# A two-layer hybrid decoder trunk: the up weights' sums in two tiles with three copies of the transferred half, and the down products added onto the residual by GpSimd

## The chip, the cores and the metric

The kernel runs on one core of a Trainium2 chip. A core has TensorE (PE in the profile; its weight loads are listed apart as PEld), VectorE (DVE), ScalarE (ACT), GpSimd (POOL) and SyncE (SP), which each work through their own instructions in order and wait for one another by semaphores. SBUF holds 128 partitions of data; PSUM holds what TensorE writes. The metric is the device time of one execution in microseconds (us). Before the change three runs took 1287.45, 1287.9 and 1292.94 us (median 1287.9).

## The reference, cut to what matters

Two layers run over 528 rows (16 learned rows ahead of 512 tokens) of width 1024. Each layer normalises, projects, mixes by two kinds of attention heads, adds the result to `h`, and then runs a gated feed-forward network, the only part that the change touches:

```python
hn = rmsnorm(h, ffn_norm_g)
ff = jax.nn.silu(jnp.einsum('bld,df->blf', hn, w_gate)) * jnp.einsum('bld,df->blf', hn, w_up)
return h + jnp.einsum('blf,fd->bld', ff, w_down)
```

`w_gate` and `w_up` are 1024 x 2816, `w_down` is 2816 x 1024, everything in float32. After the last layer `h` is normalised again and the 16 learned rows are dropped.

## The kernel before

Activations lie transposed: `h[0]` to `h[7]` are SBUF tiles of 128 features by 528 rows. Each float32 operand of a product is split into a high part of TensorE's own float32r format and a low part (the rest), and a product takes three matmuls: high by high, high by low, low by high. So each weight block needs, after it has landed, a cast on ScalarE (the high part, `whi` or `fwhi`) and a subtraction on VectorE (the low part, `wlo` or `fwlo`); `splits` (L885) does both.

**The feed-forward network.** The 2816 hidden features are 22 blocks of 128, in six rounds (`ROUNDS`). The first three blocks of a layer are computed plainly. Each of the other 19 is a `Unit`: its gate block and its up block together are a 2x2 product of half blocks, done with seven half products instead of eight (a Strassen scheme), so that sums of weight halves are needed as well as the weights. A `Down` does the same for two blocks of output features and four hidden blocks of the round before. From the third round on, units (called far) and Downs alternate, so that TensorE always has products of both kinds.

**A unit's weights.** `load` (L919) takes four transfers and adds in flight: `raw` (`t["a"]`) is the gate block, 128 x 1024; `fraw` (`t["b"]`) is the up block, onto whose first half the first half of the gate block is accumulated by a transfer of GpSimd's queue (L927); `Sw` (`t["s"]`) is a tile of 128 x 1024 of which the transfers fill the second half alone: the second half of the up block comes through SyncE (L925), and onto it a transfer of GpSimd's queue accumulates the first half (L926). `make1` to `make4` then make the four sets of split weights of the unit: `make1` from `raw`; `make2` from `Sw`, once VectorE has put the sum of its second half and of the first half of `raw` into its first half (L935), by one cast (L936) and one subtraction (L937) over 1024 columns; `make3` from `fraw`; `make4` from the last sum, which a far unit puts in `Sw`'s first half right behind L937 (L939), and another unit puts in `raw` when `make4` comes (L951). There are two `Sw` tiles, so the transfers for a unit wait until `make4` of the unit two before has read its tile. `raw` has three tiles, which Downs use too, `fraw` two. Tiles of split weights come in four pairs that jobs use in turn, and `need` (L880) asks for the next three or four jobs ahead.

**A Down's results.** `load` (L1049) fetches two blocks of `w_down` and lets GpSimd make sums of weights, six operations on 128 x 128 pieces (L1057, L1059, L1061). The products go through ScalarE copies (L1089) and VectorE sums (L1091, L1107) into a tile `S` of five rows; `add` (L1096) then adds two of these rows onto an `h` tile. For 15 of the 16 Downs of a layer this is a transfer of GpSimd's queue from `S` to `h` that accumulates (L1100); the last uses VectorE (L1102).

**What sets the order.** TensorE's order is the program's (`plan`, written out by hand). On the other engines a scheduler orders what is ready, except for pieces that are pinned or raised (`keep_in_program_order`, `high_priority`); the result is a fixed list for each engine, and whatever waits at the head of a list holds up all that stands behind it.

Of the kernel before, what the change touches and what calls it, by code (L numbers as in the profile page):

```python
# [10 lines left out]
F32 = mybir.dt.float32  # L11
F32R = mybir.dt.float32r
AF = mybir.ActivationFunctionType
ALU = mybir.AluOpType

D = 1024
NK = D // 128
# [11 lines left out]
HB = NK // 2  # L29
# [10 lines left out]
def hybrid_kernel(ctx, tc, x_t, w_in, w_fl, w_out, w_gate, w_up, w_down, vecs, b_fg, rope, decay, mask, ident, out_t):  # L40
    nc = tc.nc
# [9 lines left out]
    h = [state.tile([128, T], F32, name=f"h{k}") for k in range(NK)]  # L51
# [221 lines left out]
    def fft(tag, dt=F32R, shape=(128, T), bufs=None):  # L273
        return phase["ffn"].tile(list(shape), dt, name=tag, tag=tag, bufs=bufs)
# [519 lines left out]
    def ffn(l, st, real, last):  # L794
# [8 lines left out]
        def two(t):  # L803
            return t[:, t0:T].rearrange("p (a b) -> p a b", a=2)
# [80 lines left out]
        def splits(hi, lo, src):  # L885
            nc.scalar.copy(hi, src)  # L886
            nc.vector.tensor_sub(lo, src, hi.bitcast(F32))  # L887
# [17 lines left out]
        class Unit:  # L905
# [13 lines left out]
            def load(self):  # L919
                if "a" not in self.t:  # L920
                    for n, src, pool, tag, bufs in (("a", w_gate, wp, "raw", 3), ("b", w_up, phase["ffn"], "fraw", 2)):
                        self.t[n] = pool.tile([128, NK, 128], F32, name=tag, tag=tag, bufs=bufs)
                        nc.sync.dma_start(self.t[n], src[l, self.f])
                    s = self.t["s"] = fft("Sw", F32, (128, NK, 128), 2)
                    nc.sync.dma_start(s[:, HB:NK], w_up[l, self.f][:, HB:NK])  # L925
                    nc.gpsimd.dma_start(s[:, HB:NK], w_up[l, self.f][:, 0:HB], accum_op=ALU.add)  # L926
                    nc.gpsimd.dma_start(self.t["b"][:, 0:HB], w_gate[l, self.f][:, 0:HB], accum_op=ALU.add)  # L927

            def make1(self, hi, lo):
# [2 lines left out]

            def make2(self, hi, lo):
                a, s = self.t["a"], self.t["s"]
                nc.vector.tensor_add(s[:, 0:HB], s[:, HB:NK], a[:, 0:HB])  # L935
                nc.scalar.activation(hi, s, AF.Copy, scale=-1.0)  # L936
                nc.vector.scalar_tensor_tensor(lo, s, -1.0, hi.bitcast(F32), ALU.mult, ALU.subtract)  # L937
                if self.far:
                    nc.vector.tensor_add(s[:, 0:HB], a[:, HB:NK], s[:, 0:HB])  # L939


            def make3(self, hi, lo):
                splits(hi, lo, self.t["b"])


            def make4(self, hi, lo):
                a, s = self.t["a"], self.t["s"]
                if self.far:
                    splits(hi, lo, s[:, 0:HB])
                else:  # L950
                    nc.vector.tensor_add(a[:, HB:NK], a[:, HB:NK], s[:, 0:HB])  # L951
                    splits(hi, lo, a[:, HB:NK])

            def bank(self, n):
                def go():
# [82 lines left out]
        class Down:  # L1038
# [57 lines left out]
            def add(self, s):  # L1096
                m = 2 * self.m + s
                e = self.t["e"][:, 2 * s:2 * s + 2]
                if self.dma:
                    nc.gpsimd.dma_start(two(h[m]), e, accum_op=ALU.add)  # L1100
                else:
                    nc.vector.tensor_add(two(h[m]), e, two(h[m]))  # L1102

# [16 lines left out]
        def down_job(p, f0, f1):  # L1120

            n = f1 - f0
            t = {}

            def load():
                if t:
                    return
                t["r"] = wp.tile([128, NK, 128], F32, name="raw", tag="raw", bufs=3)
                for s in range(2):
                    nc.sync.dma_start(t["r"][:, s * n:s * n + n], w_down[l, 2 * p + s, :, f0:f1])  # L1130

            return add_job(load=load, make=lambda hi, lo: splits(hi, lo, t["r"][:, 0:2 * n]), n=2 * n)
# [40 lines left out]
        for r, (f0, f1) in enumerate(ROUNDS):  # L1173
            for f in range(f0, f1):
# [5 lines left out]
                if r > 1 and fills:  # L1180
                    p = fills.pop(0)[0]
                    if p == 0:
                        u.rest()
                        d = Down(p, r - 1, True)
# [3 lines left out]
                    else:  # L1188
                        d = Down(p, r - 1, True)
                        u.rest()  # L1190
                        d.second()
                        if f == NF - 1:
                            e = Down(fills.pop(0)[0], r - 1, False)
# [203 lines left out]
    def layer(l):  # L1397
# [80 lines left out]
        for g in range(2):  # L1478
# [15 lines left out]
                      ret_places(3, 52, 45.5, 47.5, 57.5, 55.5, 58.5, 60, 64.1, 63, 64.2))  # L1494
        plan += [op[3], op[7], op[11], op[15]] + op[16:]
        up = ffn(l, ff, real, real)
        plan += [lambda: enter("ffn"), start_ffn] + up
        return plan
# [79 lines left out]
```

## Time and profile before

| | before |
|---|---|
| runs | 1287.45, 1287.9, 1292.94 us (median 1287.9) |
| profiled execution, its own time | 1293.39 us |
| its span, first to last instruction | 1291.6 us |
| mean granted TensorE clock | 0.989 |
| busy share of the span: PE, DVE, ACT, POOL | 97%, 80%, 60%, 42% |
| DMA, mean | 132 GB/s, 170.80 MB |

A page of the profile gives busy times by engine, the span in 40 slices, the DMA queues, the chain of work that ended last and the costliest groups of instructions. Other views answer questions: the waits (who waited for whom), the chain in order of time, the timeline of an engine, one tile's or one line's instructions (minimum, median and maximum duration), and windows (busy time and number of instructions of each engine in a stretch, with the granted clock and the DMA share). L12 is line 12 of the kernel. The feed-forward network runs from about 314 to 640 us in the first layer and from about 960 to 1260 us in the second.

### The profile page before, as it was taken

How to read it: one execution, taken by the hardware profiler on the slowest of the kernel's cores; microseconds unless marked ns; L12 is line 12 of the kernel's file. 1: busy time of each engine (PE TensorE's matmuls, PEld its weight loads, DVE VectorE, ACT ScalarE, POOL GpSimd, SP SyncE). 2: the span in 40 equal slices, each digit the busy share in tenths (PEclk: the TensorE clock that was granted, in tenths of full speed). 3: DMA queues.
4: the chain of work that ended last, by engine and by line, in shares of the span. 5: the costliest groups of instructions: out<-in, count | busy, mean ns of one | idle time of the engine just before them, and what ended most of it. 6: DMA issues, size and time to landing. Idle time of an engine off the chain costs nothing. (4 is left out here: it accounts for less than half of the span.)

```text
span 1291.6 us, 25256 instructions
## 1 busy us (share of the span) xinstructions
PE 1251.1 (97%) x9463; PEld 1203.4 (93%) x9463; DVE 1032.3 (80%) x1942; ACT 780.5 (60%) x1534; POOL 544.4 (42%) x866
## 2 busy tenths in 40 slices
PE   9999999999999999899999999999999998999996
PEld 8999999999999999899899988998788998999986
DVE  7877756779678888798886877477887897999976
ACT  6666555776555556466556665457655665666654
POOL 3355645511134445355325545554102454555540
PEclk9999999999999999999999999999999999999998
DMA  6222223125776767686523232221457767778841
GB/s 216 95 78 83 83 75 91 50 87 155 175 185 151 183 165 183 145 207 165 131 75 117 70 96 82 83 79 61 139 152 182 171 162 182 180 191 193 200 104 65
DMA packets 73050, 170.80 MB, mean 132 GB/s; under 512 B 8400, under 2 KB 15312, under 8 KB 72928
## 3 DMA queue, kind: packets, MB, share of 16 engines
q1 hardware_dynamic: 50576, 128.70, 30.4%
q0 software_dynamic: 21888, 40.17, 19.3%
q8 instruction: 74, 1.21, 0.4%
q14 instruction: 48, 0.39, 0.1%
q10 hardware_dynamic: 464, 0.32, 0.1%
HBM read 146.79 MB, written 2.13 MB: 115 GB/s over the span
## 5 line engine op out<-in xcount | busy, mean ns | idle before, releaser
L194 POOL TENSOR_TENSOR wlo<-raw,whi 128x128 fp32r<-128x128 f32 x504 | 258.2, 547 | 284.7 <-ACT whi L191 284.6
L217 PE MATMUL psd<-xh,whi 128*128 128x264 f32 (+1 forms) x792 | 196.3, 315 | 0.5 <-ACT whi L191 0.5
L217 PE MATMUL psd<-xh,wlo 128*128 128x264 f32 (+1 forms) x792 | 187.1, 304 | 0.0
L217 PE MATMUL psd<-xl,whi 128*128 128x264 f32 (+1 forms) x792 | 186.6, 303 | 0.4 <-DVE xl L320 0.4
L217 PEld LDWEIGHTS psd<-xh,whi 128*128 128x128 f32 x792 | 128.8, 190 | 5.6 <-ACT whi L191 1.3
L217 PEld LDWEIGHTS psd<-xh,wlo 128*128 128x128 f32 x792 | 127.5, 189 | 6.3 <-DVE wlo L194 0.4
L217 PEld LDWEIGHTS psd<-xl,whi 128*128 128x128 f32 x792 | 128.1, 189 | 4.8 <-DVE xl L320 0.8
L191 ACT CAST whi<-raw 128x512 fp32r<-128x512 f32 (+1 forms) x168 | 98.4, 613 | 49.1 <-PE psd L217 37.0
L1100 POOL DMA_DIRECT2D h<-S x60 | 60.6, 1042 | 93.9 <-ACT S L1089 32.7
L886 ACT CAST whi<-raw 128x1024 fp32r<-128x1024 f32 (+2 forms) x68 | 62.7, 929 | 47.6 <-PE psd L898 26.1
L887 DVE TENSOR_TENSOR wlo<-raw,whi 128x1024 fp32r<-128x1024 f32 (+2 forms) x68 | 75.8, 1116 | 17.1 <-ACT whi L886 16.8
L926 POOL DMA_DIRECT2D Sw<-w_up x38 | 37.1, 975 | 111.8 <-DVE wlo L887 40.1
L898 PE MATMUL psa<-th,fwhi 128*128 128x264 f32 (+1 forms) x256 | 73.9, 289 | 1.7 <-ACT e L970 1.7
L898 PE MATMUL psa<-tl,fwhi 128*128 128x264 f32 (+1 forms) x256 | 73.4, 287 | 0.0
L898 PE MATMUL psa<-th,fwlo 128*128 128x264 f32 (+1 forms) x256 | 73.2, 286 | 0.0
L142 ACT CAST ab<-tq 128x528 fp32r<-128x528 f32 (+1 forms) x64 | 36.1, 573 | 60.4 <-DVE tq L988 31.3
L970 ACT COPY e<-psa 128x264 f32<-128x264 f32 (+1 forms) x114 | 42.7, 374 | 41.4 <-PE psa L898 41.2
L898 PE MATMUL psa<-ab,fwhi 128*128 128x264 f32 (+3 forms) x304 | 60.9, 290 | 5.7 <-ACT S L1089 5.3
L898 PE MATMUL psd<-xh,whi 128*128 128x264 f32 (+1 forms) x192 | 55.5, 289 | 8.6 <-DVE sg L980 5.4
L935 DVE TENSOR_TENSOR Sw<-Sw,raw 128x512 f32<-128x512 f32 x38 | 27.1, 713 | 45.8 <-DMA raw<-w_gate 23.3
L527 ACT ACTIVATE probs<-probs,nmax 128x144 f32<-128x144 f32 (+1 forms) x64 | 36.9, 576 | 44.4 <-DVE nmax L514 31.5
L927 POOL DMA_DIRECT2D fraw<-w_gate x38 | 33.5, 883 | 68.7 <-DVE wlo L194 21.9
(367 smaller groups left out, 4502.1 us busy)
## 6 DMA issues: line engine op xcount, KB each, us to landing
raw<-w_in SPq DMA_DIRECT2D x54, 512.0 KB, 3.5
raw<-w_gate SPq DMA_DIRECT2D x44, 512.0 KB, 5.8
fraw<-w_up SPq DMA_DIRECT2D x38, 512.0 KB, 6.1
raw<-w_down SPq DMA_DIRECT2D x64, 256.0 KB, 4.4
h<-S POOLq DMA_DIRECT2D x38, 264.0 KB, 5.7
Sw<-w_up SPq DMA_DIRECT2D x38, 256.0 KB, 3.7
fraw<-w_gate POOLq DMA_DIRECT2D x38, 256.0 KB, 4.2
Sw<-w_up POOLq DMA_DIRECT2D x38, 256.0 KB, 5.8
```

The source lines that it names most:

```text
L142: pin(nc.scalar.copy(hi, src), pinned)
L191: pin(nc.scalar.copy(hi, job["raw"][:, c0:c1]), pinned)
L194: pin(sub(lo[:, i:i + step], job["raw"][:, c0 + i:c0 + i + step], hi[:, i:i + step].bitcast(F32)), pinned)
L217: nc.tensor.matmul(ps[1][b][:, 0:c1 - c0], w[:, wk, :], x[:, c0:c1], start=(k == 0 and i == 0), stop=(k == n - 1 and i == 2))
L527: nc.scalar.activation(pr, pr, AF.Exp, bias=nmax[0:nq], scale=-1.0, accum_out=rsum)
L886: nc.scalar.copy(hi, src)
L887: nc.vector.tensor_sub(lo, src, hi.bitcast(F32))
L898: nc.tensor.matmul(bank()[:, 0:b.shape[-1]], a[:, o + k, :], b, start=(fresh and k == 0 and i == 0), stop=(k == n - 1 and i == 2), skip_gr ...
L926: nc.gpsimd.dma_start(s[:, HB:NK], w_up[l, self.f][:, 0:HB], accum_op=ALU.add)
L927: nc.gpsimd.dma_start(self.t["b"][:, 0:HB], w_gate[l, self.f][:, 0:HB], accum_op=ALU.add)
L970: nc.scalar.copy(self.t["e"][:, i], self.t["x"][:, 0:w])
L1100: nc.gpsimd.dma_start(two(h[m]), e, accum_op=ALU.add)
```

## The change

The sum of `Sw`'s second half and `raw` now goes to a tile of its own, `Sd` (128 x 512, one of it), and `Sw` keeps only the transferred half, 128 x 512, in three tiles. Together they take as much SBUF as the two tiles took. `make2` therefore casts and subtracts in two pieces of 512 columns, `make4` reads `Sd` in every unit, and `raw` is read for the last time in `make2` in every unit. In `add`, the transfer is replaced by an addition on GpSimd, from `S` and `h` in SBUF onto `h`.

```diff
-                    s = self.t["s"] = fft("Sw", F32, (128, NK, 128), 2)
-                    nc.sync.dma_start(s[:, HB:NK], w_up[l, self.f][:, HB:NK])
-                    nc.gpsimd.dma_start(s[:, HB:NK], w_up[l, self.f][:, 0:HB], accum_op=ALU.add)
+                    s = self.t["s"] = fft("Sw", F32, (128, HB, 128), 3)
+                    nc.sync.dma_start(s, w_up[l, self.f][:, HB:NK])
+                    nc.gpsimd.dma_start(s, w_up[l, self.f][:, 0:HB], accum_op=ALU.add)
                     nc.gpsimd.dma_start(self.t["b"][:, 0:HB], w_gate[l, self.f][:, 0:HB], accum_op=ALU.add)
...
             def make2(self, hi, lo):
                 a, s = self.t["a"], self.t["s"]
-                nc.vector.tensor_add(s[:, 0:HB], s[:, HB:NK], a[:, 0:HB])
-                nc.scalar.activation(hi, s, AF.Copy, scale=-1.0)
-                nc.vector.scalar_tensor_tensor(lo, s, -1.0, hi.bitcast(F32), ALU.mult, ALU.subtract)
-                if self.far:
-                    nc.vector.tensor_add(s[:, 0:HB], a[:, HB:NK], s[:, 0:HB])
-
+                d = self.t["d"] = fft("Sd", F32, (128, HB, 128), 1)
+                nc.vector.tensor_add(d, s, a[:, 0:HB])
+                for v, c in ((d, slice(0, HB)), (s, slice(HB, NK))):
+                    nc.scalar.activation(hi[:, c], v, AF.Copy, scale=-1.0)
+                    nc.vector.scalar_tensor_tensor(lo[:, c], v, -1.0, hi[:, c].bitcast(F32), ALU.mult, ALU.subtract)
+                nc.vector.tensor_add(d, a[:, HB:NK], d)
...
             def make4(self, hi, lo):
-                a, s = self.t["a"], self.t["s"]
-                if self.far:
-                    splits(hi, lo, s[:, 0:HB])
-                else:
-                    nc.vector.tensor_add(a[:, HB:NK], a[:, HB:NK], s[:, 0:HB])
-                    splits(hi, lo, a[:, HB:NK])
+                splits(hi, lo, self.t["d"])
...
                 if self.dma:
-                    nc.gpsimd.dma_start(two(h[m]), e, accum_op=ALU.add)
+                    nc.gpsimd.tensor_add(two(h[m]), e, two(h[m]))
```

TensorE's list is the same. In the changed kernel the lines L936 to L940 are `make2`, and lines from 944 of the old kernel on stand five lower (L1100 is L1095 there). The numbers in the names tell tiles apart: a higher number is a later tile.

On GpSimd's list this stood in the first layer around the second Down's additions (`fraw`, `Sw` and `raw` are the weights that come in, `S` the products, `h` the residual):

```order
L927 DMA fraw_5896<-w_gate 128x512
L1100 DMA h3_76<-S_5637 128x528
L926 DMA Sw_5898<-w_up 128x512
L1100 DMA h2_75<-S_5637 128x528
L1057 TENSOR_TENSOR sqh_5930<-raw_5927 128x128 x2
```

The same place of the changed kernel:

```order
L927 DMA fraw_5917<-w_gate 128x512
L1095 TENSOR_TENSOR h3_76<-S_5655,h3_76 128x528
L1095 TENSOR_TENSOR h2_75<-S_5655,h2_75 128x528
L926 DMA Sw_6330<-w_up 128x512
L1052 TENSOR_TENSOR sqh_5951<-raw_5948 128x128 x2
```

Before, the `fraw` and the `Sw` that stood together belonged to one unit. Now the `Sw` that stands there is that of two units later (`Sw_5919` goes with `fraw_5917`, `Sw_6124` with the unit between), and the two additions onto `h` are GpSimd's own operations of 528 columns.

On VectorE's list this stood in the first layer, at about 537 us of the span (`sg` and `e` are a unit's results on their way out of PSUM):

```order
L887 TENSOR_TENSOR fwlo_6364<-raw_6353,fwhi_6363 128x512
L935 TENSOR_TENSOR Sw_6514<-Sw_6514,raw_6510 128x512
L980 TENSOR_TENSOR sg_6381<-psd_6238,e_6236 128x528
L887 TENSOR_TENSOR fwlo_6364<-sqh_6356,fwhi_6363 128x512
L982 SCALAR_TENSOR_TENSOR sg_6381<-sg_6381,R_4293 128x528
L937 SCALAR_TENSOR_TENSOR wlo_6392<-Sw_6303,whi_6391 128x1024
```

The same place of the changed kernel:

```order
L936 TENSOR_TENSOR Sd_6420<-Sw_6330,raw_6326 128x512
L887 TENSOR_TENSOR wlo_6335<-raw_6326,whi_6334 128x1024
L887 TENSOR_TENSOR fwlo_6391<-raw_6380,fwhi_6390 128x512
L1064 TENSOR_TENSOR raw_6380<-raw_6380,sqh_6383 128x256
L975 TENSOR_TENSOR sg_6408<-psd_6265,e_6263 128x528
L887 TENSOR_TENSOR fwlo_6391<-sqh_6383,fwhi_6390 128x512
L977 SCALAR_TENSOR_TENSOR sg_6408<-sg_6408,R_4293 128x528
L939 SCALAR_TENSOR_TENSOR wlo_6419<-Sd_6420,whi_6418 128x512
L939 SCALAR_TENSOR_TENSOR wlo_6419<-Sw_6330,whi_6418 128x512
```

Before, the sum of the next unit (`Sw_6514`; the unit in work has `Sw_6303`) stood directly ahead of the step that empties PSUM (L980). Now only the sum of the unit in work stands ahead of it, and the next unit's sum comes twenty rows behind that step, after `make4`.

## The prediction

> **What bounds the kernel now.** I read the busy times first, then what TensorE waits for, then what the waited-for engine waits for, and last the stages.
>
> ```profile
> PE 1251.1 (97%) x9463; PEld 1203.4 (93%) x9463; DVE 1032.3 (80%) x1942; ACT 780.5 (60%) x1534; POOL 544.4 (42%) x866
> ```
>
> The page's first line: TensorE is busy 97% of the span, so only about 40 us can be won at all.
>
> ```profile
> PE psa L898 <- ACT S L1089: 12.1, 10, 3.6
> PE psd L898 <- DVE sg L980: 5.4, 2, 4.3
> PE psd L898 <- DVE e L973: 3.1, 2, 1.7
> ```
>
> The view of waits (who, for whom, us in total, times, longest): its largest waits lie in the feed-forward products (L898), behind ScalarE and VectorE steps that take under 1 us each. They are late for another reason:
>
> ```profile
> DVE Sw L935 <- DMA raw<-w_gate: 23.3, 8, 3.8
> DVE Sw L935 <- DMA Sw<-w_up: 22.5, 8, 6.9
> ```
>
> VectorE stands 45.8 us at L935, the sum that waits for `Sw` or `raw`, and all behind it on its list stands too. The chain of work that ended last, in order of time (start, length), shows one case:
>
> ```profile
> 1062.97 4.78 DMA Sw<-w_up
> ...
> 1068.29 7.26 DMA Sw<-w_up
> ...
> 1075.57 0.69 DVE Sw L935
> 1076.27 0.35 DVE tq L987
> ...
> 1077.98 0.28 ACT S L1089
> ...
> 1078.31 3.76 PE psa L898 x18
> ```
>
> `Sw` loads for 4.8 us, is accumulated onto for 7.3, L935 runs, and only then L987, which ScalarE and through it TensorE wait for. Followed back, the stalls of the first layer at 427, 470, 496 and 538 us lead to L935 and a late `Sw` in the same way.
>
> What these stalls cost is read from the windows (PE busy and number, PEld, DVE, ACT, POOL, then granted clock, DMA share, GB/s):
>
> ```profile
> 420.00:435.00 15.00, 12.91 (x91) 12.49 (x90) 12.09 (x20) 7.81 (x16) 7.23 (x8) 0.89 0.65 170
> 465.00:480.00 15.00, 13.65 (x110) 13.23 (x109) 11.10 (x19) 7.96 (x16) 1.77 (x3) 1.00 0.46 100
> 495.00:510.00 15.00, 13.89 (x114) 13.81 (x114) 14.97 (x25) 9.95 (x19) 8.37 (x10) 1.00 0.74 170
> 525.00:540.00 15.00, 10.53 (x79) 10.07 (x78) 7.91 (x12) 5.55 (x12) 8.03 (x8) 0.96 0.46 114
> 540.00:555.00 15.00, 15.00 (x117) 15.00 (x117) 12.94 (x21) 9.74 (x18) 6.88 (x10) 0.93 0.70 174
> 585.00:600.00 15.00, 15.00 (x126) 15.00 (x125) 14.90 (x26) 9.80 (x20) 10.30 (x10) 1.00 0.78 193
> 555.00:615.00 60.00, 60.00 (x495) 60.00 (x494) 55.94 (x88) 38.45 (x74) 33.32 (x41) 1.00 0.72 178
> 1075.00:1090.00 15.00, 11.69 (x87) 11.69 (x88) 11.57 (x19) 8.47 (x16) 3.53 (x4) 0.89 0.64 134
> 1210.00:1225.00 15.00, 15.00 (x130) 15.00 (x130) 15.00 (x26) 9.48 (x19) 9.60 (x10) 1.00 0.75 189
> 1090.00:1240.00 150.00, 149.64 (x1269) 149.08 (x1268) 143.37 (x225) 97.49 (x185) 87.91 (x104) 1.00 0.75 184
> ```
>
> An undisturbed 15 us holds 126 matmuls in the first layer (585 to 600), 130 in the second (1210 to 1225). The five disturbed stretches of the first layer hold 91, 110, 114, 79 and 117: 119 too few, at 15/126 us each 14.2 us. That of the second holds 87: 43 x 15/130 = 5.0 us. This is more than the waits themselves, since the granted clock falls to 0.89 to 0.96 around the long ones. The Trainium skill, page "TensorE: Matmul & The Clock Gate", section "What's actually happening", ties the low clock to an idle window of about 3.4 us; by that the stretch from 420 us, with no such stall, would lose no more than its idle time, 15.00 - 12.91 = 2.1 us in place of 4.2, and what follows would win 20 us in place of 22 (an estimate). The clock of 0.89 there speaks against it, and the counts decide.
>
> The same table shows the second limit: undisturbed, VectorE is busy 55.94 of 60 us and 143.37 of 150 us. It has 7% and 4% left.
>
> **The change part by part.** The sum goes against the profiled execution: 1293.4 us, of which 1291.6 are span; the shown median is 5.5 us lower.
>
> *Third copy of `Sw`.* A load may now start when `make2` of the unit three before has read its tile, not when `make4` of the unit two before has. On GpSimd's list it stands two units, some 30 us, ahead of its use, against a transfer chain of 4.8 + 7.3 = 12.1 us. So the `Sw` stalls go: 14.2 + 5.0 = 19.2 us. Next late would be `raw`, which the early units (L951) held until `make4`; `make2` now reads it last. Its two stalls are the row of L973 above, 3.1 us. They go too:
>
> ```profile
> 353.56 0.70 DVE L982 SCALAR_TENSOR_TENSOR sg<-sg,R 128x528 f32<-128x528 f32 x1
> ...
> 356.74 0.68 DVE L887 TENSOR_TENSOR wlo<-raw,whi 128x512 fp32r<-128x512 f32 x1
> ```
>
> The load that was late at 364 us was released by the second of these rows; on VectorE's new list the last reader stands just ahead of the first, some 3 us sooner, and the longest of these stalls is 1.7 us. Together **-22.3 us**. I count nothing for the wait of the new sum on the one `Sd`: on VectorE's list it stands behind the last reader.
>
> *Two halves.*
>
> ```profile
> L939 DVE TENSOR_TENSOR Sw<-raw,Sw x30: 672/680/683, 383.3 to 1236.8; 128x512 f32<-128x512 f32 x30
> ...
> L937 DVE SCALAR_TENSOR_TENSOR wlo<-Sw,whi x26: 1207/1214/1482, 335.6 to 1234.8; 128x1024 fp32r<-128x1024 f32 x26
> L886 ACT CAST fwhi<-Sw x20: 616/622/635, 410.8 to 1229.1; 128x512 fp32r<-128x512 f32 x20
> ...
> L936 ACT ACTIVATE fwhi<-Sw x12: 1056/1060/1065, 317.3 to 1201.7; 128x1024 fp32r<-128x1024 f32 x12
> ```
>
> (The view of the tile `Sw`: minimum, median, maximum in ns.) On VectorE 2 x 0.68 - 1.21 = +0.15 us a unit, for the 30 far units 4.5 us; on ScalarE 2 x 0.62 - 1.06 = +0.18 us a unit, hidden, since ScalarE is busy 10 of 15 us in the table's fullest stretch.
>
> *Additions on GpSimd.* 60 issues go, and 60 operations of 528 or 512 columns come.
>
> ```profile
> L1100 POOL DMA_DIRECT2D h<-S x60: 859/1009/1364, 405.5 to 1249.1; - x60
> ```
>
> The timeline of GpSimd and that of VectorE, near the end, where GpSimd has the one wide operation of the kernel:
>
> ```profile
> 1277.63 1.36 POOL L1285 TENSOR_TENSOR th<-th,e 128x544 f32<-128x544 f32 x1 [27.67 <-DVE e L1305]
> ```
>
> ```profile
> 1277.38 0.40 DVE L1281 TENSOR_TENSOR S<-S,sq 128x240 f32<-128x240 f32 x1
> 1277.70 0.40 DVE L1243 TENSOR_TENSOR h<-psa,h 128x240 f32<-128x240 f32 x1
> 1278.01 1.25 DVE L1281 TENSOR_TENSOR S<-S,sq 128x240 f32<-128x240 f32 x1
> ```
>
> On GpSimd itself an addition takes 1.36 us against 1.01 for the issue: +0.35, 21 us in all, hidden: GpSimd is busy 88 of 150 us. Behind a waiting addition stand the next `Sw` transfer, no longer urgent, and the next sums of `w_down`; the releasing steps are those that released the transfer.
>
> The price lies on VectorE. GpSimd runs from 1277.63 to 1278.99. A VectorE operation with one operand in PSUM (L1243) runs beside it in 0.40 us. The next, with both in SBUF, takes 1.25 us; the same operation took 0.40 us just before. So 0.85 us were waiting, until about GpSimd's end. GpSimd's pieces of 128 columns do it on a small scale (L937 at most 1482 against 1214 ns: +0.27), so an addition of 528 columns holds VectorE for up to 0.27 x 528/128 = 1.1 us. At least nothing, if it meets an idle VectorE or one with a PSUM operand. The Trainium skill, page "SBUF — State Buffer", section "SBUF: two separate sides", says that VectorE with two SBUF inputs and GpSimd exclude each other for the whole instruction; the trace agrees (0.85 us).
>
> Between 0 and 1.1 us I take 0.67. The 0.85 us is the nearest row, but there 0.38 us of the hold passed under a PSUM operation, which the additions will often meet too (two of them, L980 and L1107, stand close by on the list), and some will meet VectorE waiting for a cast. 60 x 0.67 = 40.2, with the halves 44.7 us more for VectorE in the two far stretches. It has free there, by the table, 4.06/60 of some 220 us (395 to 630, less its stalls), 14.9, and 6.63/150 of some 215 us (1030 to 1250, less its stall), 9.5: 24.4 us. Over the brim: **+20.3 us**, which TensorE must wait for, as its list cannot run ahead of its weights. In 15 us of the second layer that is 14.3 + 1.5 = 15.8 us of VectorE work.
>
> *Transfers.* 60 x 256 to 264 KB leave the queue that carries `Sw` and `fraw`; they make those land sooner. No row shows TensorE waiting for one after `Sw` is mended except `w_down` at a layer's end, so 0.
>
> Sum: 1293.4 - 22.3 + 20.3 = **1291.4**, say 1291 us, 0.2% above the median: VectorE takes the place of the late `Sw`.
>
> **The rivals.**
>
> *TensorE stays the bound.* If the additions fall into VectorE's idle time and its PSUM operations, the free 24.4 us cover them (they do up to 0.34 us an addition) and the time is 1293.4 - 22.3 = 1271 us, range 1265 to 1281. For it: a third of the hold is enough to hide, and the stretches undisturbed today had no stall with VectorE at 96%. Against: L1281.
>
> *VectorE saturated (slower).* By the whole hold of 1.1 us the work is 66 + 4.5 = 70.5 us against 24.4 free, +46.1, or 1317 us; and free time that lies in waits for casts, which come at TensorE's pace, may be usable in part only. With 0.9 us and two thirds of it: 54 + 4.5 - 16.3 = 42, or 1313 us. It makes the kernel slower by 0.5% (1294.3 us) from an addition's (1294.3 - 1271.1 + 24.4 - 4.5)/60 = 0.72 us on. For it: 1210 to 1225 has no idle VectorE at all. Its mechanism, a hold to the end of GpSimd's instruction, is what the Trainium skill's page "SBUF — State Buffer" states in the section named above.
>
> *The change doesn't do what it says.* If `Sw` still comes late, because its accumulation stands behind the additions on GpSimd, the stalls stay: about 1288 to 1293 us. Against: 30 us of lead.
>
> **How the numbers follow.** Forecast (VectorE takes most of it back; own range 1281 to 1300) 0.43, TensorE-bound 0.27, saturated 0.26, no effect 0.04. The range leaves out the lower part of the second and the upper half of the third: 1268 to 1315 us. About 0.5% is what a measurement of this kernel can tell from no change: below 1281.5 is faster, above 1294.3 slower. Faster: 0.27 and 0.03 of the forecast's; same 0.27 + 0.04; slower 0.13 + 0.26.
>
> **What would show it.** Right: no VectorE wait for `Sw` and hardly one for `raw`; operations with both operands in SBUF stretched by 0.5 to 1.1 us beside L1095; VectorE at 97% or more between 1090 and 1240; TensorE with many waits under 1 us there. Wrong: waits for `Sw` or `fraw` that stay, TensorE without waits (second case), or stretches of VectorE far from 0.67 us on the average.

## The result, and the profile after

| | before | after |
|---|---|---|
| runs | 1287.45 to 1292.94 us, median 1288.0 | 1302.55 to 1304.45 us, median 1304.3 |
| ratio, 95% interval | | 1.0104 [1.0069, 1.0140] |
| profiled execution, its own time and its span | 1293.39, 1291.6 us | 1302.55, 1300.8 us |
| mean granted TensorE clock | 0.989 | 0.994 |

The changed kernel is 1.0% slower by the recorded ratio (the medians alone stand 1.3% apart). Its time lies some 13 us above the forecast and inside the stated range, between the forecast case and the rival with VectorE saturated. The first line of the page (busy us, share of the span, number of instructions) and its row for the new additions:

```profile
PE 1249.9 (96%) x9463; PEld 1198.5 (92%) x9463; DVE 1090.7 (84%) x1980; ACT 784.9 (60%) x1572; POOL 592.6 (46%) x866
...
L1095 POOL TENSOR_TENSOR h<-S,h 128x528 f32<-128x528 f32 (+1 forms) x60 | 98.4, 1667 | 125.3 <-DVE S L1102 75.3
```

VectorE is busy 58.4 us more than before with 38 instructions more; the 60 operations of 528 columns are not on its list at all. TensorE's waits now (for whom, us in total, times, longest):

```profile
PE psd L898 <- DVE ab L143: 8.1, 6, 1.6
PE psa L898 <- DVE wlo L887: 7.9, 6, 1.4
PE psa L898 <- ACT e L965: 6.2, 7, 1.3
PE psa L898 <- ACT S L1084: 4.6, 9, 0.8
PE psd L217 <- DVE sg L834: 4.1, 2, 3.3
```

No row of the waits has L936 (the sum that was L935) waiting for `Sw` or `raw`: those 45.8 us of VectorE are gone. TensorE waits in their place for the ordinary work of VectorE and ScalarE, in many pieces of up to 1.6 us. The last row is new and stands in the plain blocks (L217), at the start of the feed-forward network. The windows (PE busy and number, PEld, DVE, ACT, POOL, then granted clock, DMA share, GB/s) show both:

```profile
310.00:325.00 15.00, 15.00 (x104) 15.00 (x104) 13.64 (x24) 8.54 (x13) 0.00 (x0) 0.81 0.21 65
395.00:630.00 235.00, 221.69 (x1776) 218.33 (x1774) 227.70 (x320) 136.97 (x269) 132.91 (x142) 0.99 0.50 130
1030.00:1250.00 220.00, 207.98 (x1724) 203.96 (x1723) 216.06 (x314) 132.65 (x262) 132.22 (x140) 1.00 0.53 137
1090.00:1240.00 150.00, 140.66 (x1163) 137.62 (x1163) 148.12 (x218) 89.49 (x178) 86.07 (x91) 1.00 0.53 136
```

Between 1090 and 1240 us, where no stall lay before, VectorE is now busy 148.12 of 150 us and TensorE gets through 1163 matmuls in place of 1269. The DMA share there fell from 0.75 to 0.53.

Why VectorE is fuller is read from two timelines of one place, VectorE's first and then GpSimd's (start, length). This is the longest kind of case:

```profile
486.00 0.69 DVE L1102 TENSOR_TENSOR S<-psd,S 128x528 f32<-128x528 f32 x1
486.61 3.78 DVE L939 SCALAR_TENSOR_TENSOR wlo<-Sd,whi 128x512 fp32r<-128x512 f32 x1
```

```profile
486.33 0.87 POOL L927 DMA_DIRECT2D fraw<-w_gate  x1
486.94 2.89 POOL L1095 TENSOR_TENSOR h<-S,h 128x528 f32<-128x528 f32 x2
```

Two additions of a Down stand one behind the other. They run from 486.94 to 489.83 us, and the VectorE subtraction that started at 486.61 ends at 490.39: 3.78 us in place of 0.68. The second addition started without letting VectorE in between.

That isn't the common case. Run e1 (below) has the same list on VectorE without GpSimd's additions, so each operation can be compared with its twin there. 58 operations that overlap an addition are longer than their twins by over 0.15 us, by 49.2 us together: 33 by about 0.5 us or less, 22 by 0.8 to 1.2 us, and three by 2.2 to 3.1 us, of which the one above is one. All but one of the 33 stand directly behind an operation with an operand in PSUM (`psa`, `psd`). The operations with an operand in PSUM are themselves not longer than in e1; the whole increase lies in the others. A place of each of the two common kinds, VectorE first:

```profile
437.57 0.70 DVE L1102 TENSOR_TENSOR S<-psd,S 128x528 f32<-128x528 f32 x1
438.19 1.21 DVE L939 SCALAR_TENSOR_TENSOR wlo<-Sd,whi 128x512 fp32r<-128x512 f32 x1
439.33 0.70 DVE L975 TENSOR_TENSOR sg<-psd,e 128x528 f32<-128x528 f32 x1
439.94 1.21 DVE L939 SCALAR_TENSOR_TENSOR wlo<-Sw,whi 128x512 fp32r<-128x512 f32 x1
```

```profile
437.18 3.42 POOL L1095 TENSOR_TENSOR h<-S,h 128x528 f32<-128x528 f32 x2 [3.75 <-ACT S L1084]
```

```profile
406.50 1.53 DVE L983 TENSOR_TENSOR tq<-e,tq 128x264 f32<-128x264 f32 x1
```

```profile
406.41 1.33 POOL L1095 TENSOR_TENSOR h<-S,h 128x528 f32<-128x528 f32 x1 [6.08 <-DVE S L1102]
```

At 437 us each addition runs beside an operation with an operand in PSUM, which keeps its 0.70 us, and then holds the subtraction behind it: 1.21 us in place of 0.68. Here VectorE does get in between the two additions. At 406 us the next operation has both operands in SBUF, meets nearly the whole addition and takes 1.53 us; the median of its line is 0.42.

The new row of L217 has another cause. The chain of work, in order of time, ahead of it:

```profile
293.76 7.96 DMA Sw<-w_up
301.72 0.02 issue
301.75 0.63 ACT fwhi L938
302.38 0.74 ACT R L295 x2
...
308.89 0.63 DVE sg L834
309.52 0.14 issue
309.66 20.34 PE psd L217 x144
```

ScalarE stands at L938, the negation of the half of `Sw` that needs no `raw`, until its transfer has landed. `R`, by which all results of the first blocks are scaled, stands behind it on ScalarE's list, PSUM is not emptied, and TensorE waits 3.3 us. The 15 us from 310 then hold 104 matmuls at a clock of 0.81.

### The profile page after: what moved, and what is told of

Its sections match the earlier page's. It is cut to its first block, busy times and chain, and to the rows that moved or that the text cites. A ratio compares the mean times of both kernels' runs of the same rounds, so it can differ in the third digit from the quotient of the medians.

```text
span 1300.8 us, 25218 instructions
## 1 busy us (share of the span) xinstructions
PE 1249.9 (96%) x9463; PEld 1198.5 (92%) x9463; DVE 1090.7 (84%) x1980; ACT 784.9 (60%) x1572; POOL 592.6 (46%) x866
## 3 DMA queue, kind: packets, MB, share of 16 engines
q8 instruction: 74, 1.21, 0.4%
## 4 chain that ended last, share of the span: by engine, by line
PE 63%; DVE 21%; issue 5%; ACT 5%; DMA 3%; POOL 2%; SPq 0%; DVEq 0%; ACTq 0%; POOLq 0%
PE psd L217 27%; PE psa L898 12%; PE psd L898 7%; PE psa L217 4%; DVE fwlo L887 3%; PE psd L1145 3%; PE psa L418 2%; DVE wlo L939 2%; PE psa L573 2%; PE psa L507 2%; DVE wlo L887 2%; DVE ab L143 1%; PE psa L730 1%; PE psa L700 1%; DMA Sw<-w_up 1%
## 5 line engine op out<-in xcount | busy, mean ns | idle before, releaser
L217 PE MATMUL psd<-xh,whi 128*128 128x264 f32 (+1 forms) x792 | 197.0, 316 | 4.6 <-DVE sg L834 4.1
L217 PE MATMUL psd<-xl,whi 128*128 128x264 f32 (+1 forms) x792 | 187.2, 304 | 0.8 <-DVE xl L320 0.7
L217 PE MATMUL psd<-xh,wlo 128*128 128x264 f32 (+1 forms) x792 | 187.5, 304 | 0.0
L1095 POOL TENSOR_TENSOR h<-S,h 128x528 f32<-128x528 f32 (+1 forms) x60 | 98.4, 1667 | 125.3 <-DVE S L1102 75.3
L217 PEld LDWEIGHTS psd<-xh,whi 128*128 128x128 f32 x792 | 129.2, 191 | 10.2 <-ACT th L142 4.7
L217 PEld LDWEIGHTS psd<-xh,wlo 128*128 128x128 f32 x792 | 127.8, 189 | 6.3 <-DVE wlo L194 0.4
L217 PEld LDWEIGHTS psd<-xl,whi 128*128 128x128 f32 x792 | 128.4, 190 | 5.5 <-DVE xl L320 1.6
L926 POOL DMA_DIRECT2D Sw<-w_up x38 | 33.5, 900 | 157.5 <-DVE fwlo L887 38.2
L886 ACT CAST whi<-raw 128x1024 fp32r<-128x1024 f32 (+1 forms) x64 | 60.4, 949 | 58.4 <-issue 22.3
L887 DVE TENSOR_TENSOR wlo<-raw,whi 128x1024 fp32r<-128x1024 f32 (+1 forms) x64 | 79.3, 1252 | 9.1 <-ACT whi L886 9.1
L407 ACT ACTIVATE sg<-sg 128x528 f32<-128x528 f32 (+1 forms) x48 | 30.7, 639 | 53.1 <-DVE sg L977 52.3
L898 PE MATMUL psd<-ab,fwhi 128*128 128x264 f32 (+1 forms) x248 | 49.9, 287 | 8.2 <-DVE ab L143 8.1
L898 PE MATMUL psa<-th,whi 128*128 128x264 f32 (+1 forms) x200 | 56.5, 282 | 0.1
```

Source lines behind the costliest of these rows:

```text
L217: nc.tensor.matmul(ps[1][b][:, 0:c1 - c0], w[:, wk, :], x[:, c0:c1], start=(k == 0 and i == 0), stop=(k == n - 1 and i == 2))
L898: nc.tensor.matmul(bank()[:, 0:b.shape[-1]], a[:, o + k, :], b, start=(fresh and k == 0 and i == 0), stop=(k == n - 1 and i == 2), skip_gr ...
L926: nc.gpsimd.dma_start(s, w_up[l, self.f][:, 0:HB], accum_op=ALU.add)
L1095: nc.gpsimd.tensor_add(two(h[m]), e, two(h[m]))
```

## The experiments

The theory that went into them: two things lose time, GpSimd's additions by holding VectorE, and the early negation; the weights' part by itself wins what was forecast. Each is compared with runs of the kernel before on the same chip beside it.

| run | weights, copies of `Sw` | additions | early negation held back | median (lowest to highest), us | ratio, 95% interval | VectorE busy, us |
|---|---|---|---|---|---|---|
| after | new, 3 | GpSimd | no | 1304.3 (1302.6 to 1304.5) | 1.0104 [1.0069, 1.0140] | 1090.7 |
| e1_weights | new, 3 | DMA | no | 1277.5 (1273.7 to 1281.8) | 0.9896 [0.9861, 0.9931] | 1037.9 |
| e2_adds | old, 2 | GpSimd | - | 1319.3 (1314.7 to 1321.7) | 1.0218 [1.0170, 1.0266] | 1091.5 |
| e3_pin | new, 3 | GpSimd | yes | 1298.2 (1295.5 to 1302.8) | 1.0059 [1.0029, 1.0088] | 1095.1 |
| e4_weights_pin | new, 3 | DMA | yes | 1266.0 (1265.0 to 1266.5) | 0.9808 [0.9767, 0.9849] | 1034.0 |
| e5_vector | new, 3 | VectorE | yes | 1284.8 (1283.5 to 1286.3) | 0.9927 [0.9898, 0.9956] | 1073.0 |
| e7_half | new, 3 | GpSimd, half of the columns | yes | 1265.1 (1264.6 to 1267.0) | 0.9785 [0.9756, 0.9814] | 1046.6 |
| e8_two_copies | new, 2 | DMA | yes | 1268.6 (1265.9 to 1270.7) | 0.9808 [0.9776, 0.9839] | 1036.3 |
| e9_pieces | new, 3 | GpSimd, in four pieces | yes | 1307.0 (1304.3 to 1311.7) | 1.0118 [1.0078, 1.0157] | 1094.8 |
| e10_weights_pin | as e4 | | | 1266.9 (1265.7 to 1270.2) | 0.9805 [0.9780, 0.9830] | 1034.9 |
| e11_two_copies | as e8 | | | 1267.3 (1266.2 to 1270.7) | 0.9809 [0.9784, 0.9834] | 1034.1 |
| e12_half_dma | new, 3 | half GpSimd, half DMA | yes | 1276.5 (1273.4 to 1279.2) | 0.9872 [0.9848, 0.9896] | 1060.1 |
| e13_two_unpinned | new, 2 | DMA | no | 1275.6 (1271.1 to 1275.9) | 0.9857 [0.9824, 0.9889] | 1035.6 |

### e1 and e2: each part alone

e1, on the changed kernel:

```diff
-                    nc.gpsimd.tensor_add(two(h[m]), e, two(h[m]))
+                    nc.gpsimd.dma_start(two(h[m]), e, accum_op=ALU.add)
```

> The changed kernel with the down products added by the accumulating DMA again, so only the weights' part of the change is left. Every engine's list is that of the changed kernel, except that 60 additions on GpSimd are DMA issues. Theory (GpSimd's additions hold VectorE, about 0.9 us each, and give back more than the third copy of Sw wins): 1273 to 1280 us, VectorE busy back near 205 us of 235 in the first far stretch, no wait of L936 for Sw, and the 3.3 us wait of TensorE at 309 us still there. Rival (the halves and the new order of VectorE's list cost the time, the additions little): 1295 us or more.

1277.5 us, 1.0% under the kernel before, as the theory has it. The lists of TensorE, VectorE and ScalarE are those of the changed kernel, so 1090.7 - 1037.9 = 52.8 us of VectorE's busy time come from additions that GpSimd carries out: 0.88 us each. They cost 1.0104 - 0.9896 = 2.1% or 27 us (e3 and e4, which are free of the early negation's waits, give 32). The rival, halves and order, is out. The figure for VectorE in the first far stretch was off (213.5 of 235 us, as more work passes in it). ScalarE's and TensorE's waits at the early negation stay, and are longer:

```profile
ACT fwhi L938 <- DMA Sw<-w_up: 15.8, 2, 9.9
...
PE psd L217 <- DVE sg L834: 9.2, 2, 6.7
```

e2 makes the reverse edit in the kernel before.

> The kernel before with the additions on GpSimd alone, two copies of Sw. Theory: the additions cost their hold also here, but part of it falls into VectorE's 45.8 us of waiting for Sw and raw: 1298 to 1312 us, with L935 still waiting for Sw. Rival (the additions cost little): 1286 to 1291 us. Second rival (GpSimd's list is what costs: the next Sw accumulation stands behind a waiting addition): over 1312 us, with longer waits of L935 for Sw than before's 22.5 us.

1319.3 us, 7 us above the theory's range. VectorE is busy 1091.5 - 1032.3 = 59.2 us more, 0.99 us an addition, and the time grows by 28.6 us, about as much as with the new weights:

```profile
DVE Sw L935 <- DMA raw<-w_gate: 24.8, 8, 4.2
...
DVE Sw L935 <- DMA Sw<-w_up: 14.2, 3, 6.5
```

VectorE still waits 39.0 us at L935 (45.8 before), so at most 6.8 us of the hold fell into these waits, less than the theory needed. Idle time at the head of a list was no free time for a hold that came at another moment; that this accounts for all of the missing 7 us is not shown. Nor are the waits longer, so the second rival is not what happened, though its number fits.

### e3 and e4: the early negation kept in program order

```diff
-                    nc.scalar.activation(hi[:, c], v, AF.Copy, scale=-1.0)
+                    pin(nc.scalar.activation(hi[:, c], v, AF.Copy, scale=-1.0), not self.far)
```

e3 makes it in the changed kernel:

> The changed kernel, with the negation of Sw of the plain and near units kept behind the instructions that stand ahead of it in the program on ScalarE. Theory: TensorE's wait at 309 us (3.3 us, and a loss of 6.3 us against the kernel before from there on) comes from ScalarE, which stands 6.7 us at that negation for a Sw transfer and holds back R; with it goes the smaller one at 949 us: 1296 to 1298 us, 6 to 8 us less than the changed kernel. Rival (the transfer delays the start of the feed-forward stage by itself, or the clock would have dropped anyway): 1302 to 1305 us.

e4 in e1:

> Both edits: additions by the accumulating DMA, and the negation of Sw of the near units kept in program order. Theory: the gains add up, 1266 to 1272 us, 1.3 to 1.7% under the kernel before. Rival (VectorE's two halves cost what the third copy wins): 1283 us or more.

e3 gives 1298.2 us, at the upper edge of its theory's range, and e4 1266.0, at the lower edge of its own. Against e1, e4 wins 11.5 us with ranges far apart. Against the changed kernel, e3 wins 0.45%, some 6 us; their intervals overlap, so that size is not secured, but the wait is gone and the same place of e3 runs at full clock:

```profile
310.00:325.00 15.00, 15.00 (x126) 15.00 (x126) 11.43 (x19) 6.54 (x9) 0.00 (x0) 1.00 0.21 62
```

126 matmuls in 15 us, 22 more than after the wait. Why the changed kernel loses less by it than e1: its second such wait, near 949 us, was 0.8 us long, e1's, near 936 us, 6.7. The first lines of the pages of e3 and then e4, which differ in the additions alone:

```profile
PE 1251.2 (96%) x9463; PEld 1198.8 (92%) x9463; DVE 1095.1 (84%) x1980; ACT 783.1 (60%) x1572; POOL 590.5 (45%) x866
```

```profile
PE 1240.3 (98%) x9463; PEld 1195.6 (95%) x9463; DVE 1034.0 (82%) x1980; ACT 784.4 (62%) x1572; POOL 557.0 (44%) x866
```

Here the additions stretch VectorE by 61.1 us, 1.02 us each, and cost 32.2 us. e4 is 1.9% faster than the kernel before; with its like, e8, e10 and e11, it is the best of all that do the whole computation.

### e5, e7 and e9: what it is about the additions

e5, on e3:

```diff
-                    nc.gpsimd.tensor_add(two(h[m]), e, two(h[m]))
+                    nc.vector.tensor_add(two(h[m]), e, two(h[m]))
```

> The changed kernel with the near units' negation of Sw in program order (e3), and the 60 additions on VectorE. Theory (what costs is VectorE's time, of which some 25 us are free in the two far stretches: in e3 its operations are stretched by about 58 us in all, and the time is 32 us over e4's): 60 additions of 0.68 us are 41 us, less 25: 1280 to 1286 us. Rival (GpSimd's waiting additions cost, by what stands behind them on its list): 1266 to 1272 us, since that list is then free of them. Second rival (VectorE's additions stand in the way of what TensorE waits for): 1295 us or more.

1284.8 us, the theory's number: with 39.0 us more of VectorE than e4 (0.65 us an addition) it lies 16 us over e8, which ran beside it and differs from e4 in the copies of `Sw` alone, a difference that cost no time (below). VectorE does these additions itself in less time than it loses when GpSimd does them. The scheduler also moved other operations on VectorE's and ScalarE's lists here, so the 16 us are not the additions' alone.

e7, on e3, with half of each addition left out:

```diff
-                    nc.gpsimd.tensor_add(two(h[m]), e, two(h[m]))
+                    nc.gpsimd.tensor_add(two(h[m])[:, 0], e[:, 0], two(h[m])[:, 0])
```

> The changed kernel with the near units' negation of Sw in program order (e3); each of the 60 additions adds the first half of its columns alone (264 or 256 in place of 528 or 512), the other half is left out. Theory (VectorE is held as long as GpSimd's instruction runs, and the first 25 us of it are free): half of 58 us is 29, less 25: 1268 to 1275 us. Rival (time is lost in proportion to the hold): half of the 32 us that e3 lies over e4, 1280 to 1284 us. Second rival (what costs is that the additions stand and wait on GpSimd's list): 1294 to 1298 us, as the waits stay.

1265.1 us, under every range: half an addition stretches VectorE by (1046.6 - 1034.0)/60 = 0.21 us, a fifth of a whole one. VectorE's timeline shows why, then GpSimd's at the same place:

```profile
473.10 0.68 DVE L887 TENSOR_TENSOR fwlo<-nwt,fwhi 128x512 fp32r<-128x512 f32 x1
473.70 0.70 DVE L1102 TENSOR_TENSOR S<-psd,S 128x528 f32<-128x528 f32 x1
474.32 0.68 DVE L939 SCALAR_TENSOR_TENSOR wlo<-Sd,whi 128x512 fp32r<-128x512 f32 x1
474.92 0.70 DVE L975 TENSOR_TENSOR sg<-psd,e 128x528 f32<-128x528 f32 x1
475.53 0.68 DVE L939 SCALAR_TENSOR_TENSOR wlo<-Sw,whi 128x512 fp32r<-128x512 f32 x1
```

```profile
473.23 2.38 POOL L1095 TENSOR_TENSOR h<-S,h 128x264 f32<-128x264 f32 x2 [0.38 <-ACT S L1084]
```

The two half additions take 2.38 us while VectorE loses nothing: L1102 and L975 have an operand in PSUM and run beside an addition, L887 and L939 read SBUF alone and keep their 0.68 us. So GpSimd waits for L887, adds beside L1102, waits for L939 and adds beside L975. A whole addition is longer than such an operation and reaches into the next one. The second rival, the waiting on GpSimd's list, is out as well: the waits stay (80.7 us for ScalarE's copies), and the time is no longer than e4's.

e9, on e3:

```diff
-                    nc.gpsimd.tensor_add(two(h[m]), e, two(h[m]))
+                    hm = two(h[m])
+                    for a in range(2):
+                        for c in (slice(0, w // 2), slice(w // 2, w)):
+                            nc.gpsimd.tensor_add(hm[:, a, c], e[:, a, c], hm[:, a, c])
```

> e3 with each addition on GpSimd cut into four of 132 or 128 columns. Theory (a VectorE operation waits for the GpSimd instruction that runs when it comes, so a short one holds it a short time): in e4 the pieces of 128 columns stretch VectorE by about 0.13 us each, four of them 0.52 us for an addition in place of 0.97: 31 us, less 25: 1268 to 1278 us. Rival (the hold is shared by columns, however they are cut): 1296 to 1302 us. Second rival (each piece makes a VectorE operation wait again, and GpSimd's own time grows): over 1302 us.

1307.0 us, the second rival's number. But VectorE is stretched by 60.8 us, no more than by whole additions, as the first rival has it; what grew is GpSimd's own time:

```profile
L1098 POOL TENSOR_TENSOR h<-S,h 128x132 f32<-128x132 f32 (+1 forms) x240 | 174.5, 798 | 112.0 <-ACT S L1084 70.8
```

Four times 798 ns are 3.2 us an addition against 1.67. That this is what puts e9 some 9 us over e3 is not shown. Short pieces one behind the other win nothing.

### e8, e10, e11 and e13: the third copy

```diff
-                    s = self.t["s"] = fft("Sw", F32, (128, HB, 128), 3)
+                    s = self.t["s"] = fft("Sw", F32, (128, HB, 128), 2)
```

e8 makes it in e4, and e13 in e1; e10 and e11 are e4 and e8 again, side by side.

> e4 (accumulating DMA, negation in program order) with two copies of Sw in place of three; only the places of Sw's load and accumulation on the two queues move, one unit later. Theory (it is the third copy that lets Sw come in time): Sw is read until make2 of the unit two before, its load then stands about one unit, some 16 us, ahead of its use against a chain of 12.1 us, with other issues between them, so part of the stalls come back: 1272 to 1282 us, with waits of L936 for Sw. Rival (that make4 reads a tile of its own is enough, the third copy wins nothing more): 1264 to 1268 us and no wait of L936 for Sw.

> The kernel of e4 again, beside the next one on the same chip. 1264 to 1268 us, 1.5 to 2.2% under the kernel before.

> The kernel of e8 (two copies of Sw) again, beside e10. If the third copy wins something of its own, 1 to 4 us over e10, with the ranges of the runs apart; if the tile of its own for make4 is all, within 1 us of e10.

> e1 (accumulating DMA, negation of Sw where the scheduler puts it) with two copies of Sw in place of three. Theory (ScalarE's stand at the early negation comes from the split of the negation into halves; the third unit's transfers beside it only lengthen it): TensorE's wait near 309 us stays, 1 to 2.5 us of it, and that near 936 us shrinks: 1268 to 1277 us. Rival (the third copy's early load causes it): no such waits, 1265 to 1268 us.

e10 and e11 give 1266.9 and 1267.3 us with ranges that overlap; the range of e8 (median 1268.6) covers both. No row of e8 or e11 has L936 waiting for `Sw`. So the third copy wins nothing that these runs can tell: the rest of the weights' part, by which `make4` reads a tile of its own and `Sw` and `raw` are free after `make2`, is enough. What the earlier release of `Sw` and that of `raw` are each worth was not separated. With two copies and the negation left early (e13), TensorE's two waits at L217 stay:

```profile
ACT fwhi L938 <- DMA Sw<-w_up: 15.1, 2, 9.1
...
PE psd L217 <- DVE sg L834: 8.5, 2, 5.9
```

So they come from the split of the negation into halves, not from the third copy's load.

### e12: half on GpSimd, half by DMA

On e3:

```diff
-                    nc.gpsimd.tensor_add(two(h[m]), e, two(h[m]))
+                    nc.gpsimd.tensor_add(two(h[m])[:, 0], e[:, 0], two(h[m])[:, 0])
+                    nc.gpsimd.dma_start(two(h[m])[:, 1], e[:, 1], accum_op=ALU.add)
```

> e3 with the first half of each addition on GpSimd and the second half by the accumulating DMA. Theory (a GpSimd addition of 264 columns fits beside the VectorE operation on PSUM that stands next to it, one of 528 does not; the DMA costs nothing): 1263 to 1268 us, the time of e7 and e4. Rival (e7 was fast because of the work it left out): 1275 us or more.

1276.5 us, the rival's number: 9.6 us over e10. The same half additions stretch VectorE by 1060.1 - 1034.9 = 25.2 us here, twice as much as in e7. The rows of L939 (minimum, median, maximum in ns) in e7 and then e12:

```profile
L939 DVE SCALAR_TENSOR_TENSOR wlo<-Sd,whi x26: 671/680/773, 335.6 to 1208.6; 128x512 fp32r<-128x512 f32 x26
```

```profile
L939 DVE SCALAR_TENSOR_TENSOR wlo<-Sd,whi x26: 671/678/1937, 336.4 to 1220.6; 128x512 fp32r<-128x512 f32 x26
```

In e7 GpSimd's idle time ahead of its additions ended 28 times with ScalarE's copy, in e12 11 times: GpSimd, with 60 issues more (60.1 us), comes to the additions later, and they start beside other operations. Operation by operation, 21 of VectorE's overlap a half addition in e7 and are longer than in e4, by at most 0.56 us and 9.9 us together; in e12 it is 26 against e10, by up to 1.8 us and 18.1 together. That the additions' moment is what counts fits this, but was not tried by itself, so the rival is not out.

## Why the prediction held, by its own steps, and where two of them fell short

**Third copy of `Sw`, -22.3 us.** The size was right: e4 and e10 lie 24.7 and 25.6 us under the kernel before, halves included, and the waits of L935 for `Sw` and `raw` went. The reason given was more than was needed: without the third copy, with a lead of one unit, the time is the same (e11). The prediction counted the lead, 30 us against a chain of 12.1, but never worked out the lead with two copies, by the estimate ahead of e8 some 16 us.

**Two halves, +0.15 us a unit on VectorE, +0.18 on ScalarE, hidden.** The durations were right and hidden. The step failed in what it left out: one half no longer needs `raw`, so the scheduler put its negation ahead, where ScalarE waited 6.7 us for the transfer with `R` behind it on its list. That costs 11.5 us without the additions (e1 against e4) and some 6 in the changed kernel. The prediction priced the halves in the far stretches alone, and put nothing for their place on ScalarE's list at the first unit, where L938 stands ahead of L295.

**Additions on GpSimd, 0.67 us each on VectorE, 40.2 us.** The mechanism was right, the term was too small: 52.8 us in the changed kernel (0.88 each), 61.1 in e3 (1.02). The value was taken down from 0.85 because part would pass beside operations on PSUM. It did: 33 operations of VectorE lost only about 0.5 us. But 22 lost 0.8 to 1.2 us, about the prediction's upper bound of 1.1, and three lost 2.2 to 3.1 us, which it did not reckon with: there the second addition of a Down ran ahead of the operation that waited. The Trainium skill, page "SBUF — State Buffer", section "SBUF: two separate sides", has whichever of the two starts first block the other for the whole instruction. The rows at 437 and 406 us agree in that VectorE waits to about the addition's end. Who gets ahead is not shown: the subtraction of 3.78 us has its recorded start 0.33 us ahead of the first addition's, and waited all the same.

**Free time of VectorE, 24.4 us.** Near in size, but not one fixed amount. The stretch less the time lost is 52.8 - 27 = 26 us in the changed kernel, 61.1 - 32.2 = 29 in e3 and 39.0 - 16 = 23 in e5, but 25.2 - 9.6 = 16 in e12. Between the same matmuls of the two far stretches (from 395 to 630 and from 1030 to 1245 us in e4), VectorE is idle for 38.7 us in e4 and 13.8 us in e3: some 25 us were taken up, and the rest was not. By the prediction's own terms 24.4 us cover 0.33 us an addition, not 0.34.

**Transfers, 0.** Right as far as the runs show: e7, without the 60 transfers, is no faster than e4 beyond the scatter of the runs, though it has half additions in their place.

**The sum.** Its terms come to -2.0 us; measured are +1.04% of the kernel before, 13 us. In per cent the runs give -1.9 for the weights (e4), +2.5 for the additions (e3 against e4) and +0.45 for the early negation (the changed kernel against e3), together +1.0. So the sum was some 15 us too low: 12 for the additions, which cost 32.2 us in place of 20.3, and about 6 for the early negation, less 2.4 that the weights won beyond their term. The forecast case's own range ended at 1300 us, and the time lies above it: the stated range holds it by the part that was given to the saturated rival. With 0.88 us an addition the prediction's sum gives 1304.0 us. That this meets the measured 1304.3 is luck in part: the sum starts from an execution some 5 us over the median and has no early negation, and these two nearly cancel. Of what was to be seen, VectorE at 148.12 of 150 us came as said, and no wait of VectorE for `Sw` or `raw` was left; TensorE's waits are up to 1.6 us, not under 1. The point from which VectorE's hold makes the kernel slower was put at 0.72 us an addition; with 0.88 it was passed, so the saturated rival's mechanism decided, at a smaller size than its 1313 us.

## What to carry to other kernels

Work moved from a DMA queue to an idle engine is not free if its operations hold up those of the engine that is nearly full: look what stands beside it on the full engine's list, operation by operation, and compare with doing the work there. When an operation is split so that one part needs fewer inputs, look where a scheduler then puts that part, and whether its input is already there when it comes up. When a change mends a late load, find the least that frees the buffer before paying for another copy.

## What the runs showed of the hardware beyond what was expected

- A hold isn't proportional to columns. Of 528 columns it was 0.88 to 1.02 us on the average, of 264 columns 0.21 us (e7) or 25.2/60 = 0.42 (e12), of four pieces of 132 together 1.01. Beside an operation of 528 columns with an operand in PSUM a half addition cost VectorE nothing (e7, at 473 us) and a whole one about 0.5 us (at 437 us); where both operands of the next operation lay in SBUF, a whole one cost about 1.1 us (at 406 us).
- GpSimd waits as well: its addition takes 1.67 us on the average against 1.36 in the row of L1285 before.
- One wait of TensorE of 3.3 us cost some 2.6 us more behind it (22 matmuls too few in the 15 us from 310): the clock was 0.81 in that stretch, which has no idle time. The far stretch from 1090 us, with its many waits of up to 1.6 us, kept a clock of 1.00. The Trainium skill, page "TensorE: Matmul & The Clock Gate", section "What's actually happening", has the clock fall after an idle window of about 3.4 us. These two rows agree with it, roughly. The stretch from 420 us of the kernel before, with 0.89 and no such wait, does not, and neither does one of the changed kernel, where TensorE's longest wait is 1.4 us:

```profile
560.00:575.00 15.00, 12.63 (x87) 11.99 (x86) 14.24 (x22) 9.35 (x19) 9.27 (x10) 0.89 0.57 148
```

So short waits can be followed by a low clock, and mostly are not; what decides it stays open.
